# The same program with its large on-chip buffers started at multiples of 128 bytes

## The chip, the cores and the metric

The kernel runs on one core of one Trainium2 chip. The metric is the device time of one execution in microseconds (us); before the change the median of three runs is 2843.84 us (2843.12 to 2845.22). TensorE (PE) does the matrix products, VectorE (DVE) and ScalarE (ACT) the elementwise work, GpSimd (POOL) a few small operations, and SyncE (SP) issues nearly all transfers from the chip's main memory (HBM) into the on-chip memory (SBUF). SBUF has 128 partitions; an address here is a byte offset within a partition, the same in all of them.

## The reference: what is computed

One decoder layer on 256 tokens of width 2048, in float32:

```python
ada = silu(c) @ ada_w + ada_b                       # nine vectors: shift, scale, gate, three times
u = modulate(rms_norm(h, norm1_g), sh1, sc1)
h = h + 0.5 * g1 * swiglu(u, ffn1_w1, ffn1_w3, ffn1_w2)      # inner width 5632
u = modulate(rms_norm(h, norm2_g), sh2, sc2)
h = h + g2 * hybrid_mixer(u, w_in, ..., w_proj_a, w_proj_b, w_out)
u = modulate(rms_norm(h, norm3_g), sh3, sc3)
h = h + 0.5 * g3 * swiglu(u, ffn2_w1, ffn2_w3, ffn2_w2)
```

The mixer projects u to 18464 columns, runs a gated DeltaNet branch (16 heads, chunks of 64 tokens) and a causal softmax branch (16 heads), merges them by two sigmoid gates after one projection each, and projects the result back.

## The kernel before

A main stream of 912 steps runs through the whole layer. A step takes 128 rows and 1024 columns of a weight matrix. Its weights land as float32 in a tile of the ring (8 tiles of 4096 bytes per partition, asked for by SP as tiles come free). `split` (L444 and after) makes two float32r parts of it: ScalarE copies the high part to `wh`, VectorE writes the rest to `wl` (4 buffers each). The activations are split in the same way. In the up-projections of both feed-forward blocks and in the input projection they are the tiles `uh` and `ul`, 16 blocks of 256 tokens each. In the down-projections, the output projection and the two branch projections they are halves of "pages": a pool of 57 tiles of 2048 bytes (`page`), which also holds nearly every other intermediate result.

A step is 12 matmuls: for each half of the tokens and each half of the columns wh with the high activations, wl with the high activations, wh with the low ones (`mm`, L453). The 512 columns of weights are the moving operand, 128 tokens of activations the stationary one, which is loaded by a LDWEIGHTS of its own before each matmul. In the profile's names `bk<-wh,uh` is: bank from moving wh and stationary uh. Units of 16 or more steps fill two or four banks. In the eight units that merge the branches (`x_proj`) the first 512 columns are a gate, with uh and ul stationary, and the second 512 a branch projection, with pages stationary: three matmuls of one kind and three of the other, in turn.

Norms, transposes, the two branches and the sums for the adaLN vectors are side work, written as generators; a rough account of the engines' times (`Clock`, `pump`) decides where each turn stands between the steps when the program is built. That account knows tile names and sizes, and no addresses. Every instruction goes through a wrapper, so most of them carry the line L184.

The order in which a tile's pool is first used sets its place in SBUF: each pool follows the one before, from the next multiple of 32 bytes. Before the change the constants come first: `con` takes 3592 bytes from 1152, which ends 8 bytes past a multiple of 128, and further small tiles follow; then the ring, the pages, `uh`, `ul`, `wh` and `wl` as the program comes to them. The starts are below; as each buffer of these pools is a multiple of 512 bytes, all buffers of a pool have the same remainder, and so has every slice of them that a float32r matmul takes.

Of the kernel before, what the change touches and what calls it, by code (L numbers as in the profile page):

```python
# [13 lines left out]
F32 = mybir.dt.float32  # L14
F32R = mybir.dt.float32r
# [54 lines left out]
def shape_constants():  # L70
    """Identity, triangles and block masks of a 128-token tile (two 64-token chunks), the one-hot
    map of distance to bucket, and the causal mask row: all from shapes alone."""
    i = np.arange(P)[:, None]
    j = np.arange(P)[None, :]
    same = (i // 64) == (j // 64)
    con = np.zeros((P, CON_W), np.float32)

    def put(name, m):
        con[:, CON[name][0]:CON[name][1]] = m

    put("ident", i == j)
    put("tri", (i <= j) & same)
    put("one0", i < 64)
    put("one1", i >= 64)
    for s in (4, 5):
        b = 1 << s
        put(f"lv{s}", ((i // (2 * b)) == (j // (2 * b))) & ((i // b) % 2 == 0) & ((j // b) % 2 == 1))
    put("eye16", np.eye(16).reshape(1, 256))
    put("incl", (i <= j) & same)
    m = np.arange(3 * P)  # L90
    dist = 2 * P - 1 - m
    d = np.maximum(dist, 0)
    half = BUCKETS // 2
    ratio = np.log(np.maximum(d, 1).astype(np.float32) / np.float32(half)).astype(np.float32)
    large = half + (ratio / np.float32(math.log(MAX_DIST / half)) * np.float32(BUCKETS - half)).astype(np.int32)
    bucket = np.where(d < half, d, np.minimum(large, BUCKETS - 1))
    hot = ((np.arange(BUCKETS)[:, None] == bucket[None, :]) & (dist >= 0)[None, :]).astype(np.float32)
    past = np.broadcast_to(np.where(dist >= 0, 0.0, NEG), (HEADS, 3 * P)).astype(np.float32)
    return {"k_con": con, "k_hot": hot, "k_past": np.ascontiguousarray(past)}
# [14 lines left out]
class Clock:  # L114
    """A rough account, in microseconds, of when the engines will have done what has been emitted: it
    decides the order in which side work is put between the steps of the main stream."""

# [7 lines left out]
    def begin(self):  # L125
        """A turn of side work: its end will be the latest end of its operations."""
        self.turn = 0.0
        self.spent = dict.fromkeys(self.spent, 0.0)
# [69 lines left out]
def tile_hybrid_layer(ctx: ExitStack, tc: tile.TileContext, A, out, dbg=None):  # L198
# [13 lines left out]
    def live():  # L212
        """Pages that something still refers to."""
        held[:] = [t for t in held if sys.getrefcount(t) > 3]
        return len(held)
# [19 lines left out]
    def set_banks(n):  # L235
        """n of the eight banks for the main stream, the others for side work."""
        while len(banks["m"]) > n:
            banks["s"].append(banks["m"].pop())
        while len(banks["m"]) < n:
            banks["m"].appendleft(banks["s"].popleft())  # L240
# [12 lines left out]
    set_banks(MB)  # L253

    def bc(ap, shape):
        return ap.to_broadcast(list(shape))

# [1 line left out]
    con = const(CON_W, "con")  # L259
# [69 lines left out]
    def heads_view(t, n=0):  # L329
        """128 x 128 per head, in DRAM."""  # L330
        return bass.AP(tensor=t.tensor, offset=t.offset + n * HG * HS, ap=[[P, P], [HS, HG], [1, P]])

    def diag_view(t, n=0):
        """The 16 x 16 blocks on the diagonals of the same."""
        return bass.AP(tensor=t.tensor, offset=t.offset + n * HG * HS, ap=[[16 * P + 16, 8 * HG], [P, 16], [1, 16]])
# [34 lines left out]

# [1 line left out]
    ring = {"out": 0, "next": 0}  # L372
    stream = []

    def ring_tile(shape):
        ring["out"] += 1
        return sb.tile(list(shape), F32, name=nm("ring"), tag="ring", bufs=RING)

    def ring_done():
        ring["out"] -= 1  # L380

# [12 lines left out]
    def load_block(q, kt, r, secs):  # L394
        """r tiles of rows of the first shift or scale or both, a block of the columns of each."""
        def load():
            lo, hi = BLOCKS[q]
            w = (hi - lo) * P
            t = ring_tile((P, r, len(secs), w))
            if r == 1:  # L400
                o = secs[0] * D + lo * P
                a = A["ada_w"]
                nc.sync.dma_start(t[:, 0, :, :], bass.AP(tensor=a.tensor, offset=a.offset + kt * P * 9 * D + o,
                                                         ap=[[9 * D, P], [D, len(secs)], [1, w]]))
                return t
            for n, sec in enumerate(secs):
                o = sec * D + lo * P
                nc.sync.dma_start(t[:, :, n, :], A["ada_w"][kt * P:(kt + r) * P, o:o + w].rearrange("(k p) n -> p k n", p=P))
            return t
        return load  # L410
# [32 lines left out]
    def split_x(src):  # L443
        """float32 [128, 256] as two float32r parts, whose sum it is."""  # L444
        t = page((P, 512), F32R)
        S.copy(t[:, 0:T], src)
        V.tensor_sub(t[:, T:2 * T], src, t[:, 0:T].bitcast(F32))
        return t
# [24 lines left out]

# [1 line left out]
    side = deque()  # L475
# [6 lines left out]
    def pump(v, s, force=False):  # L482
        """Side work that is ready and leaves VectorE and ScalarE free at times v and s."""
        for n, x in enumerate(list(side)):
# [51 lines left out]

# [1 line left out]
    def ada_load(sec, kt, half):  # L538
# [11 lines left out]
    def ada_section(sec, bias=False, ahead=None):  # L550
        ahead = ADA_AHEAD
        """silu(c) @ ada_w of one section, the sum over partitions left to TensorE."""
        acc = [page() for _ in range(4)]
# [23 lines left out]
    def ada_close(s, sec, scale, lo=0, hi=KT):  # L577
        """Adds ada_b; a scale becomes (1 + scale) * gain."""
        t = (gnT if scale else shT)[s][:, lo:hi]
# [31 lines left out]

# [1 line left out]
    def norm_sum(h, tt, n):  # L613
# [41 lines left out]
    def norm(s, last, u):  # L655
        """Emits the first part of the first tokens while `last` ends, and the others beside the first steps of unit u."""
        h = []
# [18 lines left out]

# [1 line left out]
    units = []  # L678
# [95 lines left out]

# [1 line left out]
    state = {}  # L776

    def gated(which, c, after):
        """Adds a gated part to h, half of the tokens at a time."""
        def tail(u, tt, ahead=lambda: None):  # L780
# [27 lines left out]
    def ffn(which, w1, w3, w2, begin, after, opening=None):  # L808
        """Units of one SwiGLU: up-projections of FA * 128 columns, their down-projection, the rest."""
        gT = {}  # L810
# [59 lines left out]
        def part_evac(n, q):  # L870
            """The up-projections of a quarter of the rows, added to those before it."""
            def evac(u, tt):
# [47 lines left out]

# [1 line left out]
    W_IN = A["w_in"]  # L922
# [14 lines left out]
    def heads_params():  # L937
        """beta, and the sums of log decay: per token and head, feature maps of the gates."""
        parts = []
# [98 lines left out]
    def dn_front(g, raws):  # L1038
        """Convolution, silu and l2-norms of a group of heads, feature-major."""
        xT = {}  # L1040
# [93 lines left out]
    def dn_blocks(g):  # L1134
        """(I + L)^-1 of the 16 x 16 blocks on the diagonals, one block to a partition, row by row."""
        R = [dn.setdefault(("r", g, tt), {}) for tt in range(NT)]
# [32 lines left out]
    def dn_tile(g, tt):  # L1169
        """Within the two chunks of a 128-token tile: T = (I + L)^-1, u, w, and the masked q k. The  # L1170
        keys stay as they are: their norms go into L, w and u, which are those of norm-times-v_new."""
        xT, sc = dn["x", g], dn["sc", g]
# [96 lines left out]
    def dn_scan(g):  # L1269
        """Over the four chunks: outputs and the state; then gate, norm and turn to feature-major."""  # L1270
        rk = dn["rk", g]
# [123 lines left out]
    def mb_group(g, raws):  # L1395
        """Causal softmax attention of four heads, over the one block there is."""
        ss = sb.tile([P, 16], F32, name=nm("mss"), tag="mss", bufs=2)
# [201 lines left out]

# [1 line left out]
    def opening(q, mini):  # L1601
        """A block of the rows (of the model's width) of the first OPEN up-projections."""
        if q == 0:
# [138 lines left out]
```

## Time and profile before

| | before |
|---|---|
| median of 3 runs (lowest, highest) | 2843.84 us (2843.12, 2845.22) |
| span of the profiled execution | 2845.3 us |
| PE busy | 2753.3 us, 97% |
| DVE busy | 2009.0 us, 71% |
| ACT busy | 1383.4 us, 49% |
| weight ring's DMA queue (q1) | 68.5% of 16 engines, 634.97 MB |
| chain that ended last | PE 88%, DMA 4%, DVE 3%, ACT 3% |

The span of the profiled execution, 2845.3 us, is 1.5 us (0.05%) above the median of the three times and beside the slowest of them, 2845.22 us. A matmul's row gives its duration in the pipeline, some 390 ns, although the next one starts after some 230 ns; what a matmul costs the stream is the distance between starts. The chain of waits merges matmuls that follow each other without a gap into one piece, so that a piece's time divided by its count is that distance, up to the tail of the last one.

### The profile page before, as it was taken

What the parts mean: (1) busy time and instruction counts of PE and PEld (TensorE: products, weight loads), DVE (VectorE), ACT (ScalarE), POOL (GpSimd) and SP (SyncE); (2) the same over time, 40 slices, a digit from 0 to 9 for tenths busy, and PEclk for the clock granted to TensorE, in tenths of its full rate; (3) what the DMA queues carried; (4) which work ended last, traced back from release to release, by engine and by line L of the source; (5) the groups of instructions that cost most, each with busy time, mean ns of one, the idle gap of its engine ahead of it and who ended that gap; (6) DMA issues with size and microseconds to landing.
All of it is one profiled execution on the core that took longest, in us unless ns stands there. A gap on an engine that the chain in (4) does not pass through costs nothing.

```text
span 2845.3 us, 36472 instructions
## 1 busy us (share of the span) xinstructions
PE 2753.3 (97%) x12696; PEld 2261.1 (79%) x12696; DVE 2009.0 (71%) x2778; ACT 1383.4 (49%) x2166; POOL 48.8 (2%) x43
## 2 busy tenths in 40 slices
PE   5999999999997999999999999999999999999999
PEld 4888888888876888788888888778778888888887
DVE  6699788797954775867656898889656666544545
ACT  5534454443463564554645655455564444443443
POOL 0000000000000000000100000000000000000000
PEclk9999999999998999999999999999999999999999
DMA  9898669798968664636555988989547777655654
GB/s 334 277 311 281 209 194 352 268 355 302 337 187 191 190 178 137 185 108 166 157 153 166 313 279 286 314 299 329 179 153 244 242 240 249 209 185 186 192 186 132
DMA packets 321190, 658.34 MB, mean 231 GB/s; under 512 B 44815, under 2 KB 67938, under 8 KB 321006
## 3 DMA queue, kind: packets, MB, share of 16 engines
q1 hardware_dynamic: 282432, 634.97, 68.5%
q10 hardware_dynamic: 38574, 21.05, 3.3%
q8 instruction: 99, 1.62, 0.2%
q14 instruction: 85, 0.70, 0.1%
HBM read 644.86 MB, written 11.03 MB: 231 GB/s over the span
## 4 chain that ended last, share of the span: by engine, by line
PE 88%; DMA 4%; DVE 3%; ACT 3%; issue 1%; ACTq 0%; POOL 0%; SPq 0%; DVEq 0%; POOLq 0%
PE bk L453 81%; PE bk L184 6%; DMA ring<-in_w_in 2%; DVE pg L184 2%; ACT pg L184 2%; DMA pg<-xsc 1%; DVE wl L184 1%; ACT wh L184 1%; ACT uh L184 0%; DMA ring<-in_ada_w 0%; DMA pg<-in_x 0%; ACTq L184 0%; DMA pg<-in_k_hot 0%; POOL rkq L184 0%; DMA hsp<-pg 0%
## 5 line engine op out<-in xcount | busy, mean ns | idle before, releaser
L184 DVE TENSOR_TENSOR wl<-ring,wh 128x1024 fp32r<-128x1024 f32 x912 | 1112.8, 1223 | 615.9 <-ACT wh L184 606.1
L184 ACT CAST wh<-ring 128x1024 fp32r<-128x1024 f32 x912 | 956.3, 1051 | 993.0 <-PE bk L453 829.6
L453 PE MATMUL bk<-wh,uh 128*128 128x512 f32 x2560 | 1025.1, 400 | 4.0 <-ACT uh L184 3.1
L453 PE MATMUL bk<-wl,uh 128*128 128x512 f32 x2560 | 1002.9, 392 | 1.3 <-DVE wl L184 1.2
L453 PE MATMUL bk<-wh,ul 128*128 128x512 f32 x2560 | 855.5, 392 | 2.8 <-DVE ul L184 2.8
L453 PE MATMUL bk<-wh,pg 128*128 128x512 f32 x2176 | 730.3, 395 | 3.8 <-DVE pg L184 3.2
L453 PEld LDWEIGHTS bk<-wh,ul 128*128 128x128 f32 x2560 | 482.4, 188 | 110.5 <-DVE ul L184 6.3
L453 PEld LDWEIGHTS bk<-wh,uh 128*128 128x128 f32 x2560 | 483.7, 189 | 101.7 <-ACT uh L184 4.6
L453 PEld LDWEIGHTS bk<-wl,uh 128*128 128x128 f32 x2560 | 484.2, 189 | 96.1 <-DVE wl L184 2.3
L453 PEld LDWEIGHTS bk<-wh,pg 128*128 128x128 f32 x2176 | 408.5, 188 | 101.8 <-DVE pg L184 5.1
L453 PE MATMUL bk<-wl,pg 128*128 128x512 f32 x1088 | 431.0, 396 | 0.0
L184 DVE SCALAR_TENSOR_TENSOR pg<-ring,csil,pg 128x512 f32<-128x512 f32 x552 | 388.2, 745 | 7.5 <-DMA ring<-in_ada_w 7.5
L453 PEld LDWEIGHTS bk<-wl,pg 128*128 128x128 f32 x1088 | 204.3, 188 | 49.7
L184 ACT COPY pg<-bk 128x512 f32<-128x512 f32 (+3 forms) x201 | 108.4, 563 | 191.5 <-PE bk L184 115.7
L184 DVE TENSOR_TENSOR pg<-bk,pg 128x512 f32<-128x512 f32 (+3 forms) x225 | 148.5, 676 | 46.6 <-PE bk L453 39.1
L184 DVE TENSOR_TENSOR pg<-pg,pg 128x256 fp32r<-128x256 f32 (+11 forms) x388 | 159.0, 414 | 6.5 <-ACT pg L184 1.3
L184 PE MATMUL bk<-con,pg 128*128 128x128 f32 (+2 forms) x775 | 119.2, 278 | 42.3 <-DVE pg L184 17.3
L184 PEld LDWEIGHTS bk<-con,pg 128*128 128x128 f32 (+2 forms) x775 | 96.2, 143 | 69.6 <-DMA pg<-in_ada_b 16.7
L184 PEld LDWEIGHTS bk<-pg,pg 128*128 128x128 f32 (+2 forms) x834 | 113.9, 197 | 29.4 <-issue 17.7
L184 PE MATMUL bk<-pg,pg 128*128 128x128 f32 (+3 forms) x834 | 121.7, 292 | 15.6 <-DMA pg<-xsc 13.5
L184 ACT ACTIVATE pg<-pg 128x128 f32<-128x128 f32 (+1 forms) x176 | 78.6, 450 | 50.5 <-DVE pg L184 28.3
L184 ACT ACTIVATE pg<-bk 128x128 f32<-128x128 f32 (+1 forms) x136 | 59.9, 451 | 81.5 <-PE bk L453 46.4
(110 smaller groups left out, 680.2 us busy)
## 6 DMA issues: line engine op xcount, KB each, us to landing
ring<-in_ffn_w SPq DMA_DIRECT2D x704, 256.0 KB, 4.0
ring<-in_ada_w SPq DMA_DIRECT2D x288, 512.0 KB, 5.4
ring<-in_w_in SPq DMA_DIRECT2D x512, 256.0 KB, 4.2
ring<-in_ffn_w SPq DMA_DIRECT2D x176, 512.0 KB, 4.5
ring<-in_w_in SPq DMA_DIRECT2D x34, 512.0 KB, 4.5
ring<-in_w_proj_a SPq DMA_DIRECT2D x64, 256.0 KB, 5.7
ring<-in_w_proj_b SPq DMA_DIRECT2D x64, 256.0 KB, 5.4
ring<-in_w_out SPq DMA_DIRECT2D x32, 512.0 KB, 3.9
```

The source lines that it names most:

```text
L184: r = f(*args, **kw)
L453: nc.tensor.matmul(st.unit.banks[tt, c], xs[i == 2][:, tt * P:(tt + 1) * P], w[:, c * 512:(c + 1) * 512], start=st.first and i == 0, stop= ...
```

## The change

The function `lay_out` is added and called before the first constant. It takes one tile of the ring and gives it back, takes one page and strikes it off the list of pages in use, and takes the first buffers of `uh`, `ul`, `wh` and `wl`. No instruction is issued by it; it only makes these pools the first in SBUF. The lines that define the ring's helpers move up with it, comments and docstrings become blank lines, so that line numbers shift by up to 12, and the number in each tile's name changes.

| pool | start before | remainder by 128 | start after | remainder by 128 |
|---|---|---|---|---|
| ring, 8 x 4096 | 7840 | 32 | 1152 | 0 |
| pages, 57 x 2048 | 40608 | 32 | 33920 | 0 |
| uh, 16384 | 157536 | 96 | 150656 | 0 |
| ul, 16384 | 173920 | 96 | 167040 | 0 |
| wh, 4 x 4096 | 190304 | 96 | 183424 | 0 |
| wl, 4 x 4096 | 206688 | 96 | 199808 | 0 |
| con, 3592 | 1152 | 0 | 216192 | 0 |

The small tiles behind con keep their remainders. By 256 the ring, the pages and the four parts leave 160, 160 and 96 before, and all leave 128 after. The ring's and the pages' buffers are used in the same rotation as before, which begins one buffer later. On every engine the instructions, their order and what each waits for are the same as before but for these names and line numbers.

```diff
@@ -252,10 +252,30 @@
 
     set_banks(MB)
 
+    def lay_out():
+
+        ring_tile((P, 1024))
+        ring_done()
+        held.remove(page())
+        for t in ("uh", "ul"):
+            sb.tile([P, KT, T], F32R, name=nm(t), tag=t, bufs=1)
+        for t in ("wh", "wl"):
+            sb.tile([P, 1024], F32R, name=nm(t), tag=t, bufs=LEAD + 1)
+
     def bc(ap, shape):
         return ap.to_broadcast(list(shape))
 
...
+    ring = {"out": 0, "next": 0}
+
+    def ring_tile(shape):
+        ring["out"] += 1
+        return sb.tile(list(shape), F32, name=nm("ring"), tag="ring", bufs=RING)
+
+    def ring_done():
+        ring["out"] -= 1
+
+    lay_out()
     con = const(CON_W, "con")
     nc.sync.dma_start(con[:, :P], A["k_con"][:, :P])
...
-    ring = {"out": 0, "next": 0}
     stream = []
-
-    def ring_tile(shape):
-        ring["out"] += 1
-        return sb.tile(list(shape), F32, name=nm("ring"), tag="ring", bufs=RING)
-
-    def ring_done():
-        ring["out"] -= 1
```

## Rows read from the trace of the kernel before

**Rows 1.** The page: its first part (busy time and share of the span of each engine), and the chain of work that ended last, by engine and by line.

```profile
PE 2753.3 (97%) x12696; PEld 2261.1 (79%) x12696; DVE 2009.0 (71%) x2778; ACT 1383.4 (49%) x2166; POOL 48.8 (2%) x43
...
PE 88%; DMA 4%; DVE 3%; ACT 3%; issue 1%; ACTq 0%; POOL 0%; SPq 0%; DVEq 0%; POOLq 0%
PE bk L453 81%; PE bk L184 6%; DMA ring<-in_w_in 2%; DVE pg L184 2%; ACT pg L184 2%; DMA pg<-xsc 1%; DVE wl L184 1%; ACT wh L184 1%; ACT uh L184 0%; DMA ring<-in_ada_w 0%; DMA pg<-in_x 0%; ACTq L184 0%; DMA pg<-in_k_hot 0%; POOL rkq L184 0%; DMA hsp<-pg 0%
```

**Rows 2.** The page's costliest groups: the five kinds of matmul of the main stream, with their counts, busy time and mean duration.

```profile
L453 PE MATMUL bk<-wh,uh 128*128 128x512 f32 x2560 | 1025.1, 400 | 4.0 <-ACT uh L184 3.1
L453 PE MATMUL bk<-wl,uh 128*128 128x512 f32 x2560 | 1002.9, 392 | 1.3 <-DVE wl L184 1.2
L453 PE MATMUL bk<-wh,ul 128*128 128x512 f32 x2560 | 855.5, 392 | 2.8 <-DVE ul L184 2.8
L453 PE MATMUL bk<-wh,pg 128*128 128x512 f32 x2176 | 730.3, 395 | 3.8 <-DVE pg L184 3.2
...
L453 PE MATMUL bk<-wl,pg 128*128 128x512 f32 x1088 | 431.0, 396 | 0.0
```

**Rows 3.** The chain of waits in order of time (start us, us, what): pieces of the first block's up-projection (uh and ul stationary), of its down-projection (pages stationary), and of the second block's up-projection; then, from the same view of 1600 to 1800 us, a piece of the units that merge the branches (both kinds in turn).

```profile
128.93 81.66 PE bk L453 x360
...
418.07 100.81 PE bk L453 x432
...
2287.45 40.85 PE bk L453 x180
...
1721.39 78.71 PE bk L453 x339
```

**Rows 4.** TensorE's instructions in order of time (start us, us, what): one step of a merging unit.

```profile
1760.24 0.40 PE L453 MATMUL bk<-wh,uh 128*128 128x512 f32 x1
1760.48 0.39 PE L453 MATMUL bk<-wl,uh 128*128 128x512 f32 x1
1760.70 0.40 PE L453 MATMUL bk<-wh,ul 128*128 128x512 f32 x1
1760.93 0.40 PE L453 MATMUL bk<-wh,pg 128*128 128x512 f32 x1
1761.17 0.39 PE L453 MATMUL bk<-wl,pg 128*128 128x512 f32 x1
1761.40 0.40 PE L453 MATMUL bk<-wh,pg 128*128 128x512 f32 x1
1761.63 0.40 PE L453 MATMUL bk<-wh,uh 128*128 128x512 f32 x1
```

**Rows 5.** The same view behind a gap of the mixer, and the row of that stretch among busy times by stretch (its last columns: granted TensorE clock, DMA share, GB/s).

```profile
1215.66 0.63 PE L453 MATMUL bk<-wl,uh 128*128 128x512 f32 x1
1216.09 0.63 PE L453 MATMUL bk<-wh,uh 128*128 128x512 f32 x1
1216.52 0.63 PE L453 MATMUL bk<-wl,uh 128*128 128x512 f32 x1
1216.94 1.05 PE L453 MATMUL bk<-wh,ul 128*128 128x512 f32 x2
1217.80 0.42 PE L184 MATMUL bk<-pg,pg 128*128 128x128 f32 x1
...
1215.60:1217.80 2.20, 2.20 (x7) 1.65 (x6) 2.17 (x4) 0.00 (x0) 0.00 (x0) 0.50 0.00 0
```

**Rows 6.** Busy time of PE, its weight loads, DVE, ACT and POOL by stretch (us, then count), with granted clock, DMA share and GB/s: the opening and up-projection of the first block, its down-projections, the merging and output units, and the second block.

```profile
0.00:50.00 50.00, 14.58 (x54) 11.44 (x55) 29.61 (x50) 22.72 (x49) 1.65 (x7) 0.97 0.94 337
...
200.00:300.00 100.00, 100.00 (x454) 82.98 (x453) 88.64 (x114) 41.62 (x45) 0.00 (x0) 1.00 0.84 283
...
410.00:520.00 110.00, 110.00 (x477) 88.78 (x476) 92.22 (x107) 44.35 (x48) 0.00 (x0) 1.00 0.93 338
...
540.00:640.00 100.00, 100.00 (x441) 81.62 (x440) 90.36 (x112) 42.28 (x45) 0.00 (x0) 1.00 0.92 326
...
680.00:780.00 100.00, 100.00 (x446) 81.61 (x445) 91.03 (x111) 42.40 (x50) 0.00 (x0) 1.00 0.95 343
...
1700.00:1800.00 100.00, 100.00 (x443) 81.11 (x442) 89.36 (x139) 50.98 (x83) 2.04 (x4) 1.00 0.87 290
...
1900.00:2000.00 100.00, 98.18 (x431) 79.32 (x431) 88.37 (x127) 53.67 (x85) 0.00 (x0) 1.00 0.91 324
...
2525.00:2690.00 165.00, 165.00 (x718) 133.62 (x716) 84.38 (x78) 68.02 (x71) 0.00 (x0) 1.00 0.60 189
```

**Rows 7.** Groups of instructions with their shapes kept apart, VectorE and ScalarE (busy us, mean ns of one, then idle time before).

```profile
L184 DVE TENSOR_TENSOR wl<-ring,wh 128x1024 fp32r<-128x1024 f32 x912 | 1112.8, 1223 | 615.9 <-ACT wh L184 606.1 <-DMA ring<-in_w_proj_a 1.7 <-DMA pg<-lsc 1.6
...
L184 DVE TENSOR_TENSOR pg<-pg,con 128x512 f32<-128x512 f32 x8 | 5.4, 685 | 0.0
...
L184 DVE TENSOR_TENSOR pg<-ring,pg 128x512 fp32r<-128x512 f32 x4 | 2.7, 687 | 23.3 <-ACT pg L184 23.3
...
L184 ACT CAST wh<-ring 128x1024 fp32r<-128x1024 f32 x912 | 956.3, 1051 | 993.0 <-PE bk L453 829.6 <-DMA ring<-in_ffn_w 60.5 <-DVE pg L184 23.0
...
L184 ACT CAST pg<-ring 128x512 fp32r<-128x512 f32 x4 | 2.5, 622 | 23.9 <-DMA ring<-in_w_in 23.9
```

## The prediction

> **What bounds the kernel now.** I read the page's busy times and the chain that ended last first. PE is busy 97% of the span, and 88% of the chain is PE, 81% the main stream's matmuls alone [rows 1]. DMA has 4% of the chain, DVE and ACT 3% each. So whatever the change does must show in the distance between matmul starts, or it is worth little: even a tenth off every wait for DMA would be 0.1 x 4% of 2845 us, 11 us.
>
> Next I read the chain in order of time, where a piece of gapless matmuls gives that distance. With uh and ul stationary 360 matmuls take 81.66 us and 180 take 40.85 us: 226.8 and 226.9 ns each. With pages stationary 432 take 100.81 us: 233.4 ns. In the merging units, both kinds in turn, 339 take 78.71 us: 232.2 ns [rows 3]. The single step there shows the same: six starts from 1760.24 to 1761.63 are 231.7 ns apart on average [rows 4].
>
> Last I looked for the floor. Behind a gap in the mixer, at a granted clock of 0.50 (the 1.2 GHz level, after PE had waited), five matmuls of the same shape take from 1215.66 to 1217.80, 428 ns each [rows 5]: one cycle per column of 512, and next to nothing beside it. At the full clock of 2.4 GHz the same cycles would be 214 ns. So at full clock a matmul pays 13 ns over its columns with uh, 19 ns with a page. That surplus appears only where the operands are read twice as fast, which points to the reading of SBUF. It also differs between two stationary operands that have the same shape (128 columns of 4 bytes, contiguous) and the same moving operand. The pages rotate through 57 places over 114 KB and yet a run of 432 holds one mean, so a page's far position doesn't matter. What is left as a difference is the remainder: uh and ul start 96 bytes past a multiple of 128, as wh and wl do; pages start 32 past one, 64 away from wh's. Between 226.9 and 233.4 ns lie 6.5 ns, and this is what the change touches.
>
> **The change part by part.** No engine gets, loses or moves an instruction, and no wait changes. What remains is the durations under new addresses, and I take them operand by operand.
>
> (a) Pages as stationary operand beside moving wh and wl. The remainders go from 32 beside 96 to 0 beside 0. In the trace equal remainders (uh beside wh) run at 226.9 ns, unequal ones at 233.4. I take it that the relation of the two decides and that pages fall to uh's distance. Main-stream matmuls with pages: 2176 + 1088 = 3264 [rows 2]. Of these 8 units x 16 steps x 6 = 768 stand in the merging units. The other 2496 save 233.4 - 226.9 = 6.5 ns each: 16.2 us. In the merging units all 1536 matmuls, uh's too, run at 232.2, as each is loaded beside a neighbour of the other kind; they save 5.3 ns each: 8.1 us. Sum 24.3 us. All of it is on the path: these stretches have PE busy 98 to 100% [rows 6]. Bounds: nothing (0), and down to the floor of 214 ns, 2496 x 19.4 + 1536 x 18.2 = 76 us. I take 24, as 226.9 is the row that has equal remainders.
>
> (b) uh and ul beside wh and wl: 7680 - 768 = 6912 matmuls [rows 2] with 96 beside 96 before and 0 beside 0 after. The relation stays, so I take 0. Bounds: a gain to the floor, 6912 x 12.9 = 89 us, or a loss to the distance of the pages, 6912 x 6.5 = 45 us.
>
> (c) DVE and ACT. An operand's remainder leaves no mark on them. Added from ring and page (32 beside 32) a 128x512 TENSOR_TENSOR takes 687 ns, from page and con (32 beside 0) 685. From 512 to 1024 columns, with ring (32), wh and wl (96), it goes from 687 to 1223 ns, 1.05 ns per column; ACT's cast goes from 622 to 1051, 0.84 ns per column [rows 7]. I take 0. Even 5% either way on DVE lies under PE: in the stretch where it is busiest it has 92.22 of 110 us [rows 6], so there is 16% of room.
>
> (d) Transfers into the ring and the pages, whose targets move by 32 bytes. Their packets are of 2 KB nearly all. The trace has no row for another remainder at this size. From the nearest, DMA's 4% of the chain [rows 1], 114 us, I bound it by a tenth on either side, 11 us, and take 0. A faster stream of matmuls asks for weights sooner, so I look for what is late next: in the down-projections of the first block DMA has 0.92 to 0.95 [rows 6], and 2.8% less time makes this 0.95 to 0.98. The opening runs at 0.94 as its bound, so the last of these three stretches may give back some 2 us; DVE there goes from 0.91 to 0.94.
>
> Sum against the profiled execution's own span: 2845.3 - 24.3 = 2821.0; the span stands 1.5 us above the median of the runs, and the 2 us that I let DMA give back cancel that. Forecast: 2821 us, 0.8% faster.
>
> A rule that speaks against it: the trace has stationary addresses changing the matmul's pace [rows 3]. The Trainium skill's page "SBUF — State Buffer" gives PE a second, independent read port for weight loads (section "A bandwidth-pool intuition that's wrong (but worth ruling out)") and says that PE's ports never wait on anyone (section "SBUF: two separate sides"). By that rule the sum is zero and the time 2844 us; the 6.5 ns between rows of one shape speak against it, though no row shows that low address bits are the cause.
>
> **The rivals.** 1. Nothing happens: the 6.5 ns come from something else in which pages differ, such as who wrote them or when. For it: every page in question is freshly written by ACT and DVE, while uh and ul stand for a whole projection. Against it: in the merging units pages and uh alternate within 1.4 us and the uh matmuls too are slow [rows 4], as with an effect of neighbouring operands. Time 2844 us.
>
> 2. The remainder itself costs, not the relation. [...] For it: 13 ns are missing even where the remainders are equal, and half clock shows none [rows 5]. Against it: nothing in the trace reads 512 columns of float32r from a multiple of 128. At the full floor the gain is 76 + 89 = 165 us; but 8% less time would ask DMA for 1.00 to 1.03 in the three stretches at 0.92 to 0.95 and about 0.95 to 0.99 in the merging units [rows 6]. Held at 0.95 there, some 20 us of 310 and 12 us of 400 come back: 2845 - 133 = 2712 us. With half of the surplus gone, 83 us less with no DMA bound in reach, it is 2762 us.
>
> The Trainium skill's page "TensorE: Matmul & The Clock Gate", section "Wait — 56ns, not 53.3ns?", gives columns / 2.4 GHz + 2.5 ns for back-to-back matmuls when warm, 216 ns here. The trace disagrees with it by 11 to 17 ns; were the remainders the reason, this rival would end near its full gain.
>
> 3. Slower: with all streams on one remainder, the weight loads of uh meet the moving wh at a worse place than now. The place is the up-projections and the input projection, the price 6912 x 6.5 = 45 us if they go to the pages' distance while the pages stay where they are: 2889 us. It decides from 24.3 / 6912 = 3.5 ns per matmul on. For it: how the surplus arises isn't known. Against it: uh beside wh is equal already, and equal is the faster of the two.
>
> **How the numbers follow.** Forecast (relation decides, uh unchanged) 0.48, own range 2808 to 2833 us; rival 2 in some size 0.27; rival 1 0.17; rival 3 0.08. A measurement of this kernel can tell about 0.2%, 5.7 us, from no change. Faster: 0.48 + 0.27 = 0.75; same 0.17; slower 0.08. The range reaches to rival 1 and its scatter, 2846, and down into rival 2 until about a tenth is left below, 2730 us; with the slower case outside, some 0.18 are left out.
>
> **What would show it.** Step (a): pieces of the down-projections at 227 ns per matmul in the chain, and merging units at 227 in place of 232. Step (b): the pieces of the up-projections still at 226.8; anything near 214 to 220 is rival 2, 230 or more rival 3. Steps (c) and (d): the same mean durations of the splits, and DMA at 0.95 to 0.98 in the first down-projections. I am wrong if the pages' matmuls stay at 233, or if uh's move at all.

## The result, and the profile after

| | before | after |
|---|---|---|
| median of 5 runs (lowest, highest), us | 2844.92 (2843.12, 2847.61) | 2819.69 (2811.26, 2827.0) |
| ratio of the times, with its 95% interval | | 0.9908 (0.9891 to 0.9925) |
| span of the profiled execution, us | 2845.3 | 2809.5 |

The kernel before has five runs here, the three of the table before and two more. The change makes the kernel 25.2 us faster, 0.9% (21 to 31 us by the interval); 2821 us were forecast. The profiled execution took 2811.26 us, the shortest of the five, so the two traces differ by 35.8 us and not by 25. Where the surplus stands is told below.

The page after: busy times and the chain that ended last, which answer to [rows 1].

```profile
PE 2726.4 (97%) x12696; PEld 2256.8 (80%) x12696; DVE 2008.2 (71%) x2778; ACT 1386.9 (49%) x2166; POOL 47.1 (2%) x43
...
PE 87%; DMA 5%; DVE 3%; ACT 3%; issue 1%; ACTq 0%; POOL 0%; SPq 0%; DVEq 0%; POOLq 0%
```

The counts are those of before, PE is busy 27 us less, and no other engine has taken its place in the chain: DMA goes from 4 to 5% of a shorter span, the others stay. The mean duration of one matmul says little, as the groups show that answer to [rows 2]:

```profile
L465 PE MATMUL bk<-wh,uh 128*128 128x512 f32 x2560 | 1022.6, 399 | 3.4 <-ACT uh L184 2.6
...
L465 PE MATMUL bk<-wh,pg 128*128 128x512 f32 x2176 | 719.1, 390 | 4.0 <-DVE pg L184 3.5
...
L465 PE MATMUL bk<-wl,pg 128*128 128x512 f32 x1088 | 423.6, 389 | 0.0
```

The matmuls with pages last 390 and 389 ns where they lasted 395 and 396, those with uh 399 where they lasted 400. That points to the right operand, and what the stream pays is read from the chain. Here it is after, in order of time (start us, us, what): the pieces that answer to [rows 3], and between them waits that changed.

```profile
129.06 81.64 PE bk L465 x360
...
417.98 97.96 PE bk L465 x432
...
858.58 25.84 DMA ring<-in_w_in
...
1073.30 8.34 DMA pg<-xsc
...
1192.67 7.65 DMA pg<-xsc
...
1304.52 7.42 DMA pg<-xsc
...
1426.83 6.68 DMA pg<-xsc
...
1701.24 85.04 PE bk L465 x375
...
2066.59 3.54 PE bk L465 x10
...
2258.32 40.84 PE bk L465 x180
```

Each piece, divided by its count, is now 226.8 ns: 81.64 / 360 and 40.84 / 180 with uh and ul (226.8 and 226.9 before), 97.96 / 432 with pages (233.4 before), 85.04 / 375 in the merging units (232.2 before). One distance holds in all these pieces.

What this is worth: 2496 matmuls by 233.4 - 226.8 ns is 16.5 us, 1536 by 232.2 - 226.8 is 8.3 us, together 24.8 us. That is close to the difference of the medians. It is an estimate, as it gives every matmul the distance of the long pieces; pair by pair, wherever both traces have no gap, the distances are shorter by 15.1 us with pages and 7.3 us in the merging units, 22.4 us. The other 11 us or so between the two traces stand outside the distances. These are the same places in the chain of the kernel before:

```profile
865.38 30.52 DMA ring<-in_w_in
...
1083.46 9.02 DMA pg<-xsc
...
1203.56 9.70 DMA pg<-xsc
...
1319.09 7.57 DMA pg<-xsc
...
1443.50 7.35 DMA pg<-xsc
...
2094.46 4.63 PE bk L453 x10
```

The wait for the first weights of the mixer is 30.52 - 25.84 = 4.7 us shorter, the four waits for `xsc` together 3.5 us, and ten matmuls behind a norm take 3.54 us where they took 4.63, 1.1 us. With 24.8 that makes 34.1 of 35.8 us; where the rest stands wasn't followed. The ten matmuls are a matter of the granted clock, as the rows of their stretches show, before and after (the third number from the end):

```profile
2094.40:2099.10 4.70, 4.64 (x11) 3.57 (x12) 2.33 (x5) 2.55 (x5) 2.43 (x5) 0.50 0.00 0
...
2066.50:2070.10 3.60, 3.51 (x12) 2.81 (x12) 1.23 (x4) 2.55 (x5) 2.43 (x5) 0.70 0.00 0
```

Before, all of the stretch ran at 0.50, the 1.2 GHz level; after, part of it ran at the full clock. Whether those 9.3 us belong to the change is asked by the last experiments; they don't show that any of them does.

VectorE and ScalarE, with shapes kept apart, answer to [rows 7] (busy us, mean ns of one, then idle time before):

```profile
L184 DVE TENSOR_TENSOR wl<-ring,wh 128x1024 fp32r<-128x1024 f32 x912 | 1112.9, 1223 | 597.7 <-ACT wh L184 583.4 <-DMA ring<-in_w_in 5.9 <-DMA ring<-in_ffn_w 2.2
...
L184 DVE TENSOR_TENSOR pg<-pg,con 128x512 f32<-128x512 f32 x8 | 5.4, 684 | 0.0
...
L184 ACT CAST wh<-ring 128x1024 fp32r<-128x1024 f32 x912 | 959.9, 1055 | 972.6 <-PE bk L465 794.4 <-DMA ring<-in_ffn_w 65.5 <-DVE pg L184 26.9
```

The splits take 1223 ns as before, the add 684 for 685, the cast 1055 for 1051, although every operand but `con` has moved to another remainder by 128. Busy times by stretch answer to [rows 6] (its last columns: granted clock, DMA share, GB/s). The stretches were called the first block's down-projections, but only the first is nothing else: before the change 192 of the 441 matmuls from 540 to 640 us have pages, 253 of the 446 from 680 to 780, and the others are mostly up-projection.

```profile
410.00:520.00 110.00, 110.00 (x491) 91.04 (x490) 93.88 (x109) 46.90 (x51) 0.00 (x0) 1.00 0.94 343
540.00:640.00 100.00, 100.00 (x446) 82.83 (x445) 93.10 (x116) 42.84 (x45) 0.00 (x0) 1.00 0.94 336
680.00:780.00 100.00, 100.00 (x455) 82.86 (x454) 91.05 (x113) 42.12 (x48) 0.00 (x0) 1.00 0.95 347
```

PE fills all three still, with more matmuls in each; DMA moves 1 to 3% more at 0.94 to 0.95, and PE doesn't wait for it there.

### The profile page after: what moved, and what is told of

Same layout as the page of the kernel before. It is cut to its first block, busy times and chain, and to the rows that moved or that the text cites. A ratio compares the mean times of both kernels' runs of the same rounds, so it can differ in the third digit from the quotient of the medians.

```text
span 2809.5 us, 36472 instructions
## 1 busy us (share of the span) xinstructions
PE 2726.4 (97%) x12696; PEld 2256.8 (80%) x12696; DVE 2008.2 (71%) x2778; ACT 1386.9 (49%) x2166; POOL 47.1 (2%) x43
## 4 chain that ended last, share of the span: by engine, by line
PE 87%; DMA 5%; DVE 3%; ACT 3%; issue 1%; ACTq 0%; POOL 0%; SPq 0%; DVEq 0%; POOLq 0%
PE bk L465 81%; PE bk L184 6%; DMA ring<-in_w_in 2%; DVE pg L184 2%; ACT pg L184 1%; DVE wl L184 1%; DMA pg<-xsc 1%; ACT wh L184 1%; DMA ring<-in_ada_w 0%; ACT uh L184 0%; DMA pg<-in_x 0%; ACTq L184 0%; DMA xsc<-pg 0%; DMA ring<-in_w_proj_a 0%; DMA lsc<-pg 0%
## 5 line engine op out<-in xcount | busy, mean ns | idle before, releaser
L184 DVE TENSOR_TENSOR wl<-ring,wh 128x1024 fp32r<-128x1024 f32 x912 | 1112.9, 1223 | 597.7 <-ACT wh L184 583.4
L184 ACT CAST wh<-ring 128x1024 fp32r<-128x1024 f32 x912 | 959.9, 1055 | 972.6 <-PE bk L465 794.4
L465 PE MATMUL bk<-wh,pg 128*128 128x512 f32 x2176 | 719.1, 390 | 4.0 <-DVE pg L184 3.5
L465 PE MATMUL bk<-wl,pg 128*128 128x512 f32 x1088 | 423.6, 389 | 0.0
```

Of the source, the lines that this page charges most:

```text
L184: r = f(*args, **kw)
L465: nc.tensor.matmul(st.unit.banks[tt, c], xs[i == 2][:, tt * P:(tt + 1) * P], w[:, c * 512:(c + 1) * 512], start=st.first and i == 0, stop= ...
```

## The experiments

The result leaves open what about the addresses counts. The prediction held that the difference between the stationary and the moving operand decides, by 128 bytes. One rival is that a multiple of 128 is needed, another that a start itself has a price. Each kernel below but half_load has the instructions of the kernels before and after, and differs from one of them by places alone. A "difference" is the moving operand's start less the stationary one's, in what remains by 256 bytes (the runs will show why 256): before it is 0 for uh and ul, 192 for pages; after it is 0 for both. `pad(n)` takes n bytes. Each time is a median, and each ratio is to the kernel before on the same chip, with its 95% interval. The medians of the kernel before are 2843.06 us beside pages_96, all_32, acts_64 and quarter, 2842.27 beside pages_128, rel_32, half_load and all_512, and 2843.89 beside wl_128, after_again, all_512b and all_256.

### Only the pages moved

**pages_96** is the kernel before with one edit: the pages go to where wh's remainder is, 96 by 128, and none of these pools stands at a multiple of 128. The pages move by 64 bytes, and uh, ul, wh and wl behind them by 128, all four alike.

```diff
+    ring_tile((P, 1024))
+    ring_done()
+    pad(64)
+    held.remove(page())
+    pad(64)
```

> The kernel before with 64 unused bytes ahead of the pages and 64 behind them: pages leave 96 by 128, as uh, ul, wh and wl do; ring at 32; nothing starts at a multiple of 128. Theory R (only the difference of the remainders of stationary and moving operand counts): down-projections at 226.8 ns per matmul, merging units at 226.8, as with everything at 0; about 2820 us. Theory M (a start at a multiple of 128 is what helps the pages): they stay at 233.4 and the time at 2844 us.

2820.17 us, ratio 0.9927 (0.9909 to 0.9946). The chain:

```profile
417.94 97.97 PE bk L462 x432
...
1712.98 85.04 PE bk L462 x375
```

226.8 ns in both kinds of stretch: the whole gain of the change, without any of these pools at a multiple of 128. The pages stand 256 bytes from wh here by 512, so a difference of 256 counts as none.

**all_32** shifts all pools of the changed kernel by 32 bytes.

```diff
     def lay_out():
+        pad(32)
         ring_tile((P, 1024))
```

> The changed kernel with 32 unused bytes ahead of the ring: ring, pages, uh, ul, wh, wl all leave 32 by 128. Theory R: every piece at 226.8 ns per matmul, about 2820 us. Theory S (the stationary operand's own remainder counts: 32 is slow, 96 and 0 are not): uh and pages both at 233.4, 6912 x 6.5 + 24 = 69 us more, about 2889 us. Theory M: pages back at 233.4, 2844 us.

2822.16 us, ratio 0.9936 (0.9917 to 0.9954):

```profile
128.65 81.65 PE bk L469 x360
...
417.57 97.98 PE bk L469 x432
```

226.8 ns again. A start has no price of its own, in these two kernels.

### Differences that are not zero

**acts_64** moves uh and ul by 64 and wh and wl by 128 bytes: differences 64 (uh, ul) and 128 (pages).

```diff
         held.remove(page())
+        pad(64)
         for t in ("uh", "ul"):
             sb.tile([P, KT, T], F32R, name=nm(t), tag=t, bufs=1)
+        pad(64)
```

> The changed kernel with 64 unused bytes ahead of uh and 64 behind ul: uh and ul leave 64 by 128, ring, pages, wh and wl 0. Theory R: the up-projections take the place of the down-projections at 233.4 ns, down-projections stay at 226.8, merging units go to 232; 6912 x 6.5 + 8 = 53 us more than with everything at 0, about 2873 us. Theory S: uh at 226.8 if 64 is a good remainder, about 2820 us.

2850.52 us, ratio 1.0025 (1.0000 to 1.0050):

```profile
129.44 82.42 PE bk L470 x360
...
420.69 100.79 PE bk L470 x432
...
1728.52 86.89 PE bk L470 x375
```

uh and ul pay, as they should, though 228.9 and not 233 ns. But the pages run at 233.3 ns with all of them at wh's remainder by 128. The theory by 128 fails here; 256 is the next period to try.

**quarter** gives differences 96 (uh, ul) and 160 (pages).

```diff
+        pad(96)
         held.remove(page())
+        pad(64)
         for t in ("uh", "ul"):
             sb.tile([P, KT, T], F32R, name=nm(t), tag=t, bufs=1)
+        pad(96)
```

> The changed kernel with pages at 96 by 128, uh and ul at 32, ring, wh and wl at 0: no instruction differs. Theory R: up-projections show a difference of 32 (stationary past moving), down-projections one of 96; none was measured yet: between 226.8 and 233.4 ns, 230 for both if the distance to the nearer equal place counts, about 2856 us. Theory S: uh at 32 goes to 233.4, pages at 96 stay at 226.8, about 2873 us.

2879.44 us, ratio 1.013 (1.008 to 1.018):

```profile
130.51 84.00 PE bk L471 x360
...
426.65 101.20 PE bk L471 x432
...
1739.05 87.10 PE bk L471 x375
```

233.3 ns with uh and ul, 234.3 with pages. Now all of the stream pays, and the kernel is 36 us slower than before. The size was off on both theories.

**pages_128** keeps every pool at a multiple of 128 and moves the pages alone to difference 128; what stands behind them moves by 256 bytes, which counts as nothing by 256. It puts the change's own description to the test.

```diff
+        pad(128)
         held.remove(page())
+        pad(128)
```

> The changed kernel with 128 unused bytes ahead of the pages and 128 behind them: every pool still starts at a multiple of 128, but by 256 the pages leave 0 while uh, ul, wh and wl leave 128. Theory R128 (the difference by 128 counts): down-projections stay at 226.8 ns, about 2820 us. Theory R256 (the difference by 256 counts, as the down-projections of the run with uh at 64 suggest: 232.8 ns with wh 128 past the page by 256): down-projections at about 233, merging units at 232, 2496 x 6 + 1536 x 5 = 23 us more, about 2843 us.

2834.62 us, ratio 0.996 (0.9934 to 0.9986):

```profile
128.34 81.66 PE bk L470 x360
...
417.55 100.40 PE bk L470 x432
...
1710.97 86.94 PE bk L470 x375
```

226.8 ns with uh and ul as after the change, but 232.4 with pages and 231.8 where both alternate: nearly the distances of before. By distances alone 2496 x 5.6 + 1536 x 5.0 = 21.7 of the 24.8 us are lost again, and 3.1 us should be left; the median is 7.7 us below before, and the ratio's interval puts the gain at 4 to 19 us. What is above 3.1 us stands outside the distances and stays open. So multiples of 128 are not what helps; the period is 256, with which pages_96, equal by 256 and not by 512, agrees.

**rel_32** asks for a place better than equal: differences 32 (uh, ul) and 224 (pages), 32 bytes to either side.

```diff
+        pad(128)
         ring_tile((P, 1024))
         ring_done()
+        pad(32)
         held.remove(page())
+        pad(192)
         for t in ("uh", "ul"):
             sb.tile([P, KT, T], F32R, name=nm(t), tag=t, bufs=1)
+        pad(32)
```

> The changed kernel with pads so that by 256 wh and wl start 32 past uh and ul, and 224 past the pages. Theory R256 with the distances measured so far (0: 226.8 ns, 64: 229, 96 to 192: 233 to 234): up-projections between 226.8 and 229, down-projections between 226.8 and 233.4, about 2840 us. Theory F (equal is not the best place; single intervals of 224 and 226 ns stood in the runs at 64 and 96): one of the two falls below 226.8 ns, and the time below 2820 us.

2876.39 us, ratio 1.0109 (1.007 to 1.0148):

```profile
131.43 84.00 PE bk L472 x360
...
427.46 100.79 PE bk L472 x432
...
1739.30 87.52 PE bk L472 x375
```

233.3, 233.3 and 233.4 ns. 32 bytes cost nearly as much as the worst place, 234.3 ns; the cost doesn't grow with the difference, and no place tried beats equal.

**wl_128** moves wl alone: in each group of three, the matmul with moving wl has difference 128 and the two with wh have 0.

```diff
         for t in ("wh", "wl"):
+            if t == "wl":
+                pad(128)
             sb.tile([P, 1024], F32R, name=nm(t), tag=t, bufs=LEAD + 1)
+        pad(128)
```

> The changed kernel with 128 unused bytes between wh and wl: two of three matmuls have their moving operand at the stationary operand's place by 256 (wh), the third (wl) 128 past it. If the pace is set by stationary and moving operand: the third that reads wl goes from 226.8 to about 232.4 and drags little of the rest, 228.7 ns on average, 10944 x 1.9 = 20 us more, about 2840 us. If only the place of all moving operands against each other mattered, uh and pages alike would go to 232 or more: 10944 x 5.6 = 61 us, 2881 us.

2854.37 us, ratio 1.004 (1.0025 to 1.0055):

```profile
130.17 83.43 PE bk L471 x360
...
424.21 99.45 PE bk L471 x432
...
1723.44 87.51 PE bk L471 x375
```

The direction was right, the size was not: 231.8, 230.2 and 233.4 ns, and 230.5 in the second block's up-projection (41.49 us for 180 matmuls). A third of the matmuls with a 6 ns surplus would make 228.8. Either the odd third makes its neighbours pay too, as the uh matmuls of the merging units did before [rows 4], or the place of wl against wh counts by itself; this run doesn't separate the two.

### Half as much to load

**half_load** keeps the changed kernel's places and loads 64 of the 128 stationary columns in all but a unit's first and last steps. It leaves out half of the products of those steps.

```diff
-        nc.tensor.matmul(st.unit.banks[tt, c], xs[i == 2][:, tt * P:(tt + 1) * P], w[:, c * 512:(c + 1) * 512],
+        half = P if st.first or st.last else P // 2
+        nc.tensor.matmul(st.unit.banks[tt, c][:half, :], xs[i == 2][:, tt * P:tt * P + half], w[:, c * 512:(c + 1) * 512],
```

> The changed kernel with half of each stationary operand left out: in all steps but the first and the last of a unit a matmul loads 64 tokens and writes 64 partitions, so half of the products are not computed. Moving operands, counts and places are those of the changed kernel. Theory L (the weight load's reads delay the moving operand's): the 13 ns above 213.3 fall to about half, 220 ns per matmul, and the time to about 2755 us. Theory P (a fixed cost of each matmul): 226.8 ns and 2820 us.

2841.85 us, ratio 0.9993 (0.9977 to 1.0009):

```profile
129.19 82.22 PE bk L466 x360
...
419.87 99.33 PE bk L466 x432
```

228.4 and 229.9 ns, longer by 1.6 and 3.2 ns than with 128 columns. The loads did get shorter. Here are those with uh in the changed kernel and in half_load (busy us, mean ns of one, then idle time before):

```profile
L465 PEld LDWEIGHTS bk<-wh,uh 128*128 128x128 f32 x2560 | 483.1, 189 | 99.4 <-ACT uh L184 4.2 <-ACT wh L184 1.0 <-issue 0.6
...
L466 PEld LDWEIGHTS bk<-wh,uh 128*64 128x64 f32 x2048 | 276.3, 135 | 175.7 <-issue 1.6 <-ACT wh L184 0.7
```

So 54 ns less of loading took nothing off the distance. Both expectations miss. The 13 ns that are left over the columns' 214 are not a price per stationary column; what they are stays open.

### The absolute start, and the waits

**all_512** and **all_256** shift all pools of the changed kernel, by 384 bytes to a multiple of 512 and by 128 to one of 256. **all_512b** is all_512 again, beside **after_again**, the changed kernel unaltered.

```diff
     def lay_out():
+        pad(384)
         ring_tile((P, 1024))
```

> The changed kernel with 384 unused bytes ahead of the ring: every pool starts at a multiple of 512 in place of 128 past a multiple of 256. Theory R256: the differences are the same, so 226.8 ns everywhere and about 2820 us. Theory B (the 13 ns over 512 columns at 2.4 GHz are paid for starting off a multiple of 256): down towards 214 ns, 10944 x 13 = 140 us less at most, DMA-bound stretches taken off: 2700 to 2760 us.

> The changed kernel once more, unaltered, beside the next two on the same chip. 226.8 ns in every piece and 2820 us, 2811 to 2827 as at first.

> The run with everything at a multiple of 512 again: it came out some 15 us below the changed kernel with the same distance between matmuls, and the difference lay in the wait for the transfers at the start of the mixer. Theory C (that wait varies by itself, and the run drew the short one): 2820 us like the changed kernel. Theory D (where transfers start, 128 past a multiple of 256 or at one, changes that wait): 2805 us again.

> The changed kernel with 128 unused bytes ahead of the ring: every pool at a multiple of 256 that is none of 512. All distances as before, so 226.8 ns per matmul. Theory C: 2820 us. Theory D: 2805 us, as with multiples of 512.

| kernel | us (lowest, highest) | ratio (95% interval) |
|---|---|---|
| all_512 | 2804.93 (2804.13, 2814.29) | 0.987 (0.9841 to 0.99) |
| after_again | 2821.08 (2808.38, 2823.74) | 0.9915 (0.9893 to 0.9936) |
| all_512b | 2811.56 (2799.52, 2827.54) | 0.9879 (0.9851 to 0.9908) |
| all_256 | 2814.2 (2797.66, 2823.59) | 0.9889 (0.9858 to 0.992) |

The distance is 226.8 ns in all four. all_512 has a lower median than the changed kernel with the same distance, so the difference stands elsewhere. Its chain has a shorter wait:

```profile
418.99 97.96 PE bk L469 x432
...
871.62 18.84 DMA ring<-in_w_in
```

and that of all_512b, the same program:

```profile
417.33 97.98 PE bk L469 x432
...
860.69 30.50 DMA ring<-in_w_in
```

The wait for the mixer's first weights is 18.84 us in one execution and 30.50 in another of the same kernel, on another chip. The trace of after_again, which is the changed kernel itself, has this:

```profile
418.21 97.98 PE bk L465 x432
...
859.47 29.36 DMA ring<-in_w_in
...
2076.61 4.63 PE bk L465 x10
```

Its wait is 29.36 us, where the first trace of the changed kernel had 25.84 and before 30.52, and its ten matmuls take 4.63 us again. So the 4.7 and the 1.1 us by which the traces of before and after differ here are not shown to be the change's. Nor are the 3.5 us of the waits for `xsc`: the four sum to 30.0 us in after_again and 30.1 in the first trace, but to 33.0 in all_32 and 34.2 in pages_96, which have the same distances, and 33.6 before. With these waits back and a mean granted clock of 0.991 as before (0.995 in the first trace), after_again's span is 2821.9 us, 23.4 below that of before: this pair differs by about what the distances are worth. Run beside each other, the changed kernel, all_256 and all_512b have intervals that overlap; whether a start at 256 or 512 is worth some us stays open, and neither is shown to beat the change. Six executions of all_512b on one chip go from 2799.52 us at a mean granted clock of 0.995 to 2827.54 at 0.989; which of the two, the clock or the waits, leads the other wasn't tested.

### The distances together

| difference by 256 | ns from start to start | seen in |
|---|---|---|
| 0 | 226.8 | uh and ul before, in pages_128; all after, in pages_96, all_32, all_256, all_512, after_again |
| 32 | 233.3 | uh and ul in rel_32 |
| 64 | 228.9 | uh and ul in acts_64 |
| 96 | 233.3 | uh and ul in quarter |
| 128 | 232.4, 233.3 | pages in pages_128, acts_64 |
| 160 | 234.3 | pages in quarter |
| 192 | 233.4 | pages before |
| 224 | 233.3 | pages in rel_32 |

But for 0, each difference was seen with one kind of stationary operand alone, from pieces of the first block; acts_64's pages, for one, run at 232.5 ns in the second block (55.79 us for 240).

One more rival can be settled from the traces kept. ScalarE and VectorE write wh and wl while other buffers of these pools are read, so it could be the writing that meets the pages, and not the reading of the moving operand. In the trace of the kernel before, the gapless distances between page matmuls with neither writing in between have a mean of 233.8 ns (271 of them), those with VectorE writing wl throughout 233.4 (670), with ScalarE writing wh 233.3 (652). The surplus is there without the writes.

## Why the prediction was right, step by step

**(a) Pages fall to uh's distance.** Right in size, and in its mechanism as far as it says that the relation of the two operands decides. Forecast were 226.9 ns in the down-projections and the merging units, and 24.3 us; measured were 226.8 in both, 24.8 us by distances of the long pieces (22.4 pair by pair) and 25.2 between medians. pages_96 gets it by moving the pages against the others, without the change's order of pools, so that the rest of the change adds nothing that shows.

One step was inexact, and that the forecast came out all the same is luck: "The remainders go from 32 beside 96 to 0 beside 0", taken by 128. pages_128 and acts_64 show that equal remainders by 128 don't suffice, and pages_96 that equal ones by 256 do. The forecast holds because the change puts all these pools at 128 by 256. Had it placed them at multiples of 128 that are not equal by 256, the same argument would have promised 24 us, and some 3 would have come by distances, as in pages_128 (7.7 between its medians).

**(b) uh and ul unchanged.** Right: 226.8 ns before and after. Rival 3 priced their loss at 45 us; that the loss exists was right, quarter and rel_32 have it at 233.3 ns and end 36 and 34 us behind the kernel before, with pages that are no faster than before. The change avoids it since uh and wh stay equal.

**(c) VectorE and ScalarE.** Right: the splits, adds and casts differ by at most 4 ns.

**(d) Transfers.** Nothing was given back where I let 2 us go: from 680 to 780 us PE has no gap. The forecast DMA share of 0.95 to 0.98 was too high; it came out at 0.94 to 0.95. Two of the three stretches it was taken from hold up-projections too, which don't get faster. "No wait changes" holds for what each instruction waits for; how long the waits last differs from one execution to the next by more than the 2 us at issue here.

**The rivals.** Rival 1, something else in the pages: refuted by pages_96, whose instructions are those of before and in which only the starts differ, by 64 bytes for the pages and by 128 for uh, ul, wh and wl; pages_128 differs from the changed kernel in the pages' remainder by 256 alone and brings most of the surplus back. Rival 2, the remainder itself: refuted by all_32, all_256 and all_512, which hold 226.8 ns with the pools started 32, 128 and 384 bytes further on; a start that isn't a multiple of 32 wasn't tried. Rival 3 didn't occur.

The Trainium skill's page "SBUF — State Buffer", sections "A bandwidth-pool intuition that's wrong (but worth ruling out)" and "SBUF: two separate sides", has weight loads read through a port of their own that waits on nobody. By that rule every kernel with pads alone would have one time; the runs go from 226.8 to 234.3 ns per matmul and from 0.987 to 1.013 of the time before, so here the measurement decides against it. How the surplus arises stays open. That the reads of the two operands collide is argued from the relation of their starts, and no run shows it: half_load, whose shorter loads should have eased it, didn't.

The page "TensorE: Matmul & The Clock Gate" of the Trainium skill, section "Wait — 56ns, not 53.3ns?", makes 216 ns of 512 columns. No piece of 100 or more matmuls in any run here comes below 226.7; all of them load a stationary operand before each matmul, in float32r.

## What to carry to other kernels

Where PE is the bound, divide gapless pieces of the chain by their counts and compare pieces that differ in one operand only: 6.5 ns out of 230 stood in the trace here, while mean durations hid them. Where float32r matmuls load a stationary operand each, start both operands' pools equal by 256 bytes and read the distances again when a pool is added: 32 bytes to either side made rel_32 1.1% slower than the kernel before and 2% slower than the changed one. The aim is equality by 256, and not a multiple of 128 or 256.

## What the runs showed that was not expected

- Equal remainders by 128 are not enough: pages at difference 128 run at 232.4 to 233.3 ns, at 0 and at 256 at 226.8.
- The surplus doesn't grow with the difference. It is 6.5 ns at 32 and at 96 bytes, but only 2.1 at 64.
- One matmul in three with another difference (wl_128) costs 3 to 7 ns on the mean of all three, where a third of 6 ns would be 2.
- Half of the stationary columns make a load 54 ns shorter, and the distance between matmuls 1.6 to 3.2 ns longer.
- One wait of one program differs by 11.7 us between two executions on two chips (18.84 and 30.50 us), a third of what separates the spans of before and after.
